# A token shift between two transformer blocks: from on-chip transfers to products with a shifted diagonal

## The chip, the cores and the metric

The program runs on one core of one Trainium2 chip. The metric is the device time of one execution in microseconds (us), as the median of several runs.

The engines, as the profile names them: PE (TensorE) multiplies matrices, PEld is its load of the stationary operand; DVE (VectorE) and ACT (ScalarE) compute element by element; POOL (GpSimd) does so too; SP (SyncE) only issues transfers. Each engine executes its own queue in order. SBUF is the on-chip memory of 128 partitions, PSUM the accumulators that PE writes.

## The reference, cut to what matters

Two blocks run one after the other on 256 tokens of width 1024. The second block has two layers; each begins with a mixer of four branches over one input projection, `x @ w_in`, and ends with a feed-forward (in layer 1 a mixture of eight experts). The second branch is recurrent, and it begins with a shift by one token: every token's 1024 projected columns are mixed with those of the token before it.

```python
def mixer_block(x, w_in, ...):
    p_swa, p_rwkv, p_fox, p_dsa, p_gate = split_cols(x @ w_in, IN_GROUPS)
    o_swa = swa_branch(*split_cols(p_swa, SWA_SPLITS), sinks)
    o_rwkv = rwkv7_branch(p_rwkv, mu, w0, w_up, ...)
    ...

def rwkv7_branch(p, mu, w0, w_up, a0, a_up, g_up, ...):
    p_prev = jnp.pad(p[:, :-1], ((0, 0), (1, 0), (0, 0)))
    p = p + mu * (p_prev - p)
    r, k, v, w_lo, a_lo, g_lo = split_cols(p, RWKV_SPLITS)
    ...
```

## The kernel before, in words

Activations lie token-major in two blocks of 128 tokens, t = 0 and 1, a token to a partition. A product (`gemm_tok`, L289) streams its weight from DRAM in pieces of at most 2048 columns. `wload` (L217) takes a piece into a buffer of the ring `raw` (three buffers, issued on SP, L222), and splits it in two parts: ACT casts the high part `whi` (L230), DVE subtracts it from the piece for the remainder `wlo` (L233). Each has a ring of four buffers. PE then makes three products per 128 rows of the weight: high by high (L323), remainder by the input's high part (L324), high by the input's low part (L325). So PE waits for ACT and DVE, these wait for the loads, and a new load waits for the remainder made from the buffer it will overwrite.

The mixer (`block2_mixer`, L1475) first projects the recurrent branch's 1024 columns, `p_rwkv`; `proj` evacuates them from the accumulators, block 0 by DVE (L1495), block 1 by ACT (L1493). Next come the projection of `p_swa` (768 columns, two banks of 384), two gates of 1024 columns and the other projections. The branches themselves are generators: `later` (L526) queues one, and `step` (L530) runs a piece of it whenever the products have consumed some weight, so their instructions stand between the products on each engine. The order on an engine comes from the order in which the program is written and from priorities that the framework gives; it is fixed when the program is built.

The recurrent branch (`rwkv`, L1194) has two tiles `pv`, one per block, for the token before. A memset clears row 0 of the first (L1205); three transfers on ACT's queue then move `p_rwkv` down by one partition: rows 0 to 126 of block 0 (L1206), its last row into row 0 of block 1 (L1207), and rows 0 to 126 of block 1 (L1208). When they have landed, L1219 subtracts, L1220 multiplies by `mu`, L1221 adds: for columns 768 to 1023 (the low-rank parts) all on DVE, for columns 0 to 767 the subtraction on DVE and the rest on POOL. The low-rank parts go through two activations (L1223, L1224) and a tensor-scalar (L1225), are transposed on PE (L1067, into `loT`), and multiplied by the small weights `ups` (L1237 to L1239). Later steps are `kk` and `sq` on POOL (L1271, L1273), which share that queue with `dup` (L1079) of the `p_swa` branch.

`mi` (L143) gives one of four PSUM banks for all such small products. The identity matrix for the transposes, `identr`, is a constant of 128x128 (L95 to L99). For the mixture of experts `moe_loads` (L1673) loads the router's weight `rw` and the constants `tri` and `iota` into a pool of that stage; `iota` is compared with ranks in L1776.

Of the kernel before, what the change touches and what calls it, by code (L numbers as in the profile page):

```python
# [26 lines left out]
def host_constants():  # L27
    c = {}
    c["ident"] = np.eye(P)
# [40 lines left out]
# small vectors of a layer of the second block, laid side by side  # L70
# [4 lines left out]
def layout(inputs):  # L75
    """The arrays of the launch: the inputs, and some of them once more laid out for fewer transfers."""
# [8 lines left out]
class Net:  # L85
    def __init__(self, ctx, tc, a, out, dump=None):
# [8 lines left out]
        self.identr = self.cp.tile([P, P], F32R, name="identr")  # L95
        self.ident = self.identr.bitcast(F32)
        t = self.sp.tile([P, 512], F32, name="c_ident", tag="xt", bufs=3)[:, :P]
        self.nc.gpsimd.dma_start(t, a["consts"][:, COFF["ident"][0]:sum(COFF["ident"])])
        self.nc.vector.tensor_copy(self.identr, t)  # L99
# [12 lines left out]
    def in_turn(self, dst, src):  # L112
        """A load behind the ones of the weights that came before it."""
        self.tc.keep_in_program_order(self.nc.sync.dma_start(dst, src))
# [31 lines left out]
    @staticmethod  # L146
    def staged(items):
        """items: lists of as many emitters; stage s of an item comes along with stage 0 of the s-th next. A generator."""
        n = len(items[0])
        for i in range(len(items) + n - 1):  # L150
            for s in range(n):
                if 0 <= i - s < len(items):
                    items[i - s][s]()
            yield

    def pipeline(self, items):
        for _ in self.staged(items):
            pass

    def rsqrt(self, v, n):  # L160
        """1/sqrt(v) for a [P, n] tile of float32."""
# [14 lines left out]
    def rsqrt1(self, v):  # L176
        """1/sqrt(v) for a tile [P, 3] of v, v / 4, v / 16: steps w' = (w w v / s - 3) w, with s the square of w's own
        factor, -2 for each; the last takes the factor -8 out."""
# [22 lines left out]
    def ring(self, tag, shape, dt):  # L201
        """A tile of the ring of that tag; more_rings, of (pool, slots by tag), add to it."""
# [9 lines left out]
    def prefetch(self, w, c0, cw, n=1):  # L212
        """Loads and splits the first n pieces of the weight of the next product ahead of their turn."""
# [3 lines left out]
    def wload(self, src, n, cw, f0):  # L217
        """Loads a piece of a weight, n columns from f0 on of its rows of cw laid end to end, and splits it in two
        float32r parts; a list of (row, first column, end, hi, lo) with hi(column, width), lo(column, width)."""
# [21 lines left out]
    def plan(w, c0, cw):  # L241
        """w: list of [P, nk, N] views; pieces of at most 2048 columns: whole rows, or any part of rows that lie end to end."""
# [16 lines left out]
    def pieces(self, w, c0, cw, pre=None):  # L259
        """Yields the parts of the pieces; pre() is traced after the first, and the vector engine's part  # L260
        of the second queues behind it."""
# [27 lines left out]
    def gemm_tok(self, lhs, w, c0, cw, toks, evac, tail=1, head=1, pre=None, nxt=None):  # L289
        """Token-major product: out[t] [128, cw] = sum_k lhs(k, t)^T w[k]; evac(t, column, width, psum).  # L290
        Through the first head and last tail pieces of the weight the first block of tokens goes ahead; pre(t) comes
        before the first use of block t; nxt: weight, column and width of the next product, to be loaded ahead."""
# [7 lines left out]
        for i, parts in enumerate(self.pieces(w, c0, cw, pre is not None and (lambda: pre(toks[0])))):  # L300
            # the last piece for the blocks behind the first one
# [32 lines left out]
    def gemm_feat(self, rhs, w, c0, cw, evac, pre=None):  # L334
        """Feature-major product: out[j] [128, 512 tokens] for each 128 columns of w; evac(j, psum). With pre the
        first two pieces go by halves of the tokens, and pre(half) comes before the first use of a half."""
# [35 lines left out]
    def turn4(self, z, K, k0):  # L372
        """Transposes of z [P, K*128] by feature = K*p + k, for four k's at most from k0 on."""
# [5 lines left out]
    def to_feat(self, z, K, hi, lo, affine=None, turned=None):  # L379
        """z [P, K*128] token-major -> hi/lo [P, K, 128] with feature = K*p + k.  # L380
        affine(k) -> (scale, shift) per-feature columns; shift may be None."""
# [20 lines left out]
    def rms_sum(self, ss, src, h, junk):  # L402
        """ss[:, h] <- sum of the squares of half h of src."""
# [10 lines left out]
    def rms_z(self, src, out):  # L414
        """out <- src [P, D] / its root mean square."""
# [6 lines left out]
    def close_rms(self, hs, gate, z):  # L422
        """evacuation of a residual product: hs[t] += gate(t) * product, then z(t) <- hs[t] / its root mean square."""
# [12 lines left out]
    def ln_var(self, st):  # L436
        """mean, and variance and eps in the form of rsqrt1, of the statistics st of the two halves."""
# [28 lines left out]
    def busy(self, n):  # L466
        """n products that nothing needs, which keep the tensor engine's clock up while loads are waited for."""
# [4 lines left out]
    def ada_lambda(self):  # L472
        nc, a = self.nc, self.a
        # lambda of the differential attention on all partitions
# [15 lines left out]
    def ada(self, l, s, norm=None):  # L490
        """mods[l, s] [P, 8, 2] <- segment s of the modulation of layer l, feature-major, for c and c_ctx;
        with norm: (1 + it) times that gain. A generator, one piece of the weight per step."""
# [37 lines left out]
    def step(self, n=1):  # L530
        """Runs n steps (may be a fraction, which adds up) of the work that was put off."""
# [12 lines left out]
    def gate_rows(self, l, s, c, out):  # L544
        """out [P, D] <- mods[l, s] of condition c on all partitions, by way of DRAM."""
# [1442 lines left out]
```

## Time and profile before

| | us |
|---|---|
| median of 3 runs | 2547.35 |
| lowest, highest run | 2543.98, 2552.41 |
| span of the profiled execution | 2546.3 |
| PE busy | 2356.2 (93%) |
| DVE busy | 1497.3 (59%) |
| ACT busy | 1065.1 (42%) |
| POOL busy | 298.6 (12%) |
| mean granted clock of PE | 0.953 of 2.4 GHz |

The span reaches from the first to the last instruction of one profiled execution; its own time as a run is not given apart from it, and the span lies within the range of the three runs. Busy shares are averages over stages with different limits; which wait ends last is read from the chain and the timelines. In a timeline row stand the start, the duration, the engine, the line, the operation, what it writes and reads, how many such rows were merged, and in brackets the idle time before it and what ended that.

### The profile page before, as it was taken

To read this page: it belongs to the slowest core of one execution; us is meant where nothing else is said; L and a number is where in the kernel's file an instruction comes from. 1 tells how busy PE (TensorE), PEld (TensorE's weight loads), DVE (VectorE), ACT (ScalarE), POOL (GpSimd) and SP (SyncE) were. 2 spreads that over 40 slices of the span, in tenths; PEclk is the share of its full clock that TensorE was granted. 3 is DMA by queue.
4 is the path that set the end of the run, shared out by engine and by line. 5 is a ranking of instruction groups with operands and counts; after the bars stand their busy time and mean duration, and the time that the engine had idled before them with its cause. 6 is when DMAs were issued, how large, how long until landed. Compare 5 with 4: busy or idle time off the path is not lost.

```text
span 2546.3 us, 33113 instructions
## 1 busy us (share of the span) xinstructions
PE 2356.2 (93%) x13136; PEld 1900.2 (75%) x13138; DVE 1497.3 (59%) x2473; ACT 1065.1 (42%) x1684; POOL 298.6 (12%) x242
## 2 busy tenths in 40 slices
PE   8899999999998999975999989974999979999996
PEld 4567877777776878854787768864787768889885
DVE  4247732322366565455566765464566778898887
ACT  3137432222235544432354344422344437666773
POOL 1100000000002000012101210022100322122222
PEclk8899999999999999997999999986999989999998
DMA  8581344544331065523244445622334438888994
GB/s 285 149 198 60 99 146 136 174 149 141 116 111 59 26 235 165 203 98 114 93 133 156 156 160 164 208 97 86 114 108 155 157 114 321 298 320 289 333 336 161
DMA packets 122067, 421.47 MB, mean 166 GB/s; under 512 B 11060, under 2 KB 16180, under 8 KB 100912
## 3 DMA queue, kind: packets, MB, share of 16 engines
q1 hardware_dynamic: 114128, 401.32, 45.8%
q0 software_dynamic: 4816, 15.27, 2.3%
q10 hardware_dynamic: 2960, 2.68, 0.3%
q8 instruction: 105, 1.72, 0.3%
q14 instruction: 58, 0.48, 0.1%
HBM read 416.08 MB, written 1.07 MB: 164 GB/s over the span
## 4 chain that ended last, share of the span: by engine, by line
PE 79%; DVE 9%; DMA 4%; issue 3%; POOL 2%; ACT 1%; ACTq 1%; SPq 0%; POOLq 0%; DVEq 0%
PE acc L323 17%; PE acc L324 17%; PE acc L325 17%; PE acc L356 3%; PE acc L357 3%; PE acc L358 3%; DMA pv<-p_rwkv 3%; DVE wlo L233 2%; PE mi L1029 2%; PE mi L517 2%; PE mi L506 2%; PE mi L1336 1%; PE mi L376 1%; PE mi L1784 1%; PE mi L985 1%
## 5 line engine op out<-in xcount | busy, mean ns | idle before, releaser
L233 DVE TENSOR_TENSOR wlo<-raw,whi 128x1024 fp32r<-128x1024 f32 (+2 forms) x648 | 802.1, 1262 | 495.9 <-ACT whi L230 493.5
L230 ACT CAST whi<-raw 128x1024 fp32r<-128x1024 f32 (+2 forms) x692 | 672.8, 1010 | 792.5 <-PE acc L325 574.5
L324 PE MATMUL acc<-wlo,xh 128*128 128x512 f32 (+3 forms) x1184 | 463.5, 392 | 81.4 <-DVE wlo L233 81.3
L323 PE MATMUL acc<-whi,xh 128*128 128x512 f32 (+3 forms) x1184 | 466.9, 399 | 28.0 <-ACT whi L230 22.3
L325 PE MATMUL acc<-whi,xl 128*128 128x512 f32 (+3 forms) x1184 | 460.1, 389 | 1.0 <-DVE xl L370 1.0
L324 PEld LDWEIGHTS acc<-wlo,xh 128*128 128x128 f32 x1184 | 230.4, 195 | 127.9 <-DVE wlo L233 91.9
L323 PEld LDWEIGHTS acc<-whi,xh 128*128 128x128 f32 x1184 | 230.5, 195 | 78.0 <-ACT whi L230 23.9
L325 PEld LDWEIGHTS acc<-whi,xl 128*128 128x128 f32 x1184 | 229.8, 194 | 39.5 <-issue 2.4
L324 PE MATMUL acc<-wlo,hh 128*128 128x512 f32 x528 | 208.9, 396 | 0.0
L323 PE MATMUL acc<-whi,hh 128*128 128x512 f32 x528 | 208.9, 396 | 0.0
L325 PE MATMUL acc<-whi,hl 128*128 128x512 f32 x528 | 208.3, 395 | 0.3 <-DVE hl L370 0.3
L323 PE MATMUL acc<-whi,gh 128*128 128x384 f32 (+3 forms) x512 | 172.8, 337 | 2.0 <-DVE yl L1848 2.0
L325 PE MATMUL acc<-whi,gl 128*128 128x384 f32 (+3 forms) x512 | 170.3, 333 | 0.0
L324 PE MATMUL acc<-wlo,gh 128*128 128x384 f32 (+3 forms) x512 | 170.0, 332 | 0.0
L233 POOL TENSOR_TENSOR wlo<-raw,whi 128x1024 fp32r<-128x1024 f32 x44 | 108.7, 2470 | 344.7 <-ACT whi L230 344.7
L356 PE MATMUL acc<-xh,whi 128*128 128x512 f32 (+1 forms) x384 | 148.0, 387 | 0.0
L357 PE MATMUL acc<-xl,whi 128*128 128x512 f32 (+1 forms) x384 | 147.2, 384 | 0.0
L358 PE MATMUL acc<-xh,wlo 128*128 128x512 f32 (+1 forms) x384 | 147.0, 384 | 0.0
L323 PEld LDWEIGHTS acc<-whi,hh 128*128 128x128 f32 x528 | 100.0, 189 | 26.5 <-issue 4.2
L325 PEld LDWEIGHTS acc<-whi,hl 128*128 128x128 f32 x528 | 100.1, 190 | 22.7 <-DVE hl L370 0.7
L324 PEld LDWEIGHTS acc<-wlo,hh 128*128 128x128 f32 x528 | 99.9, 189 | 21.6
L323 PEld LDWEIGHTS acc<-whi,gh 128*128 128x128 f32 x512 | 97.0, 189 | 11.4 <-DVE yl L1848 2.5
(574 smaller groups left out, 3225.9 us busy)
## 6 DMA issues: line engine op xcount, KB each, us to landing
raw<-in_exp_w_dram SPq DMA_DIRECT2D x120, 1024.0 KB, 5.8
raw<-in_ada_w_dram SPq DMA_DIRECT2D x48, 1024.0 KB, 5.2
raw<-in_w_in_dram SPq DMA_DIRECT2D x40, 1024.0 KB, 4.9
raw<-in_ffn_w_in_dram SPq DMA_DIRECT2D x32, 1024.0 KB, 5.2
raw<-in_ffn_w_dram SPq DMA_DIRECT2D x27, 1024.0 KB, 4.9
raw<-in_ffn_w_out_dram SPq DMA_DIRECT2D x19, 1024.0 KB, 5.0
raw<-in_exp_w_dram SPq DMA_DIRECT2D x24, 512.0 KB, 4.8
raw<-in_even_w_in_dram SPq DMA_DIRECT2D x10, 1024.0 KB, 5.4
```

What stands on the lines that cost most here:

```text
L230: nc.scalar.copy(hi, s)
L233: e.tensor_tensor(out=lo, in0=s, in1=hi.bitcast(F32), op=OP.subtract)
L323: nc.tensor.matmul(o, xh, hi(c, m), start=k == 0, stop=False)
L324: nc.tensor.matmul(o, xh, lo(c, m), start=False, stop=False)
L325: nc.tensor.matmul(o, xl, hi(c, m), start=False, stop=k == K - 1 and c + m == b + bw)
L356: nc.tensor.matmul(o, wh, xh[:, n0:n1], start=k == 0, stop=False)
L357: nc.tensor.matmul(o, wh, xl[:, n0:n1], start=False, stop=False)
L358: nc.tensor.matmul(o, wl, xh[:, n0:n1], start=False, stop=k == K - 1)
L376: self.nc.tensor.transpose(pt[:, j * P:(j + 1) * P], z[:, k0 + j::K], self.ident)
L506: nc.tensor.matmul(ps[32 * j:32 * j + 32, :], self.ct[:, 4 * g + j, :], v[:, j, :], start=g == 0, stop=g == 1, tile_position=(0, 32 * j))
L517: nc.tensor.matmul(pf[rw, 2 * k:2 * k + 2], mod[:, k::KD], self.sel2, start=True, stop=True, tile_position=(0, 64 * h))
L1029: nc.tensor.matmul(po[:, (h - c0) * 64:(h - c0) * 64 + 64], aT[:, j * P:(j + 1) * P], v(h, jj), start=jj == 0, stop=jj == nkb - 1)
```

## The change

The constant `ident` becomes `diag`, 128x264, with ones on a diagonal that starts at column 8. Three windows of it are used: from column 8 on the identity as before; from column 7 on a diagonal shifted by one (`shift[0]`); from column 135 on a matrix with a single one (`shift[1]`), which takes the last row of block 0 to the first row of block 1. The memset and the three transfers are gone. A new inner function `shifted` multiplies parts of `p_rwkv` by these windows in float32 into a bank of `mi`, and the subtraction reads that bank: 1 bank for columns 768 to 1023 of both blocks, 3 banks for the rest. The windows and the subtractions of columns 0 to 767 are cut to what fits a bank, so there are nine products and six subtractions per layer. All subtractions of a group of columns come ahead of its multiplications.

Two small edits go with it: the router's weight is loaded into a buffer of the ring `xt`, and `iota` is kept in bfloat16, loaded by way of the same ring and cast. (The diff also drops comments, so that lines of the changed kernel have other numbers; these are left out here.)

```diff
-    c["ident"] = np.eye(P)
+    c["diag"] = np.eye(P, P + 136, 8)
...
-        self.identr = self.cp.tile([P, P], F32R, name="identr")
+        diag = self.cp.tile([P, P + 136], F32R, name="diag")
+        t = self.sp.tile([P, 512], F32, name="c_diag", tag="xt", bufs=3)[:, :P + 136]
+        self.nc.gpsimd.dma_start(t, a["consts"][:, COFF["diag"][0]:sum(COFF["diag"])])
+        self.nc.vector.tensor_copy(diag, t)
+        self.identr = diag[:, 8:8 + P]
         self.ident = self.identr.bitcast(F32)
-        t = self.sp.tile([P, 512], F32, name="c_ident", tag="xt", bufs=3)[:, :P]
-        self.nc.gpsimd.dma_start(t, a["consts"][:, COFF["ident"][0]:sum(COFF["ident"])])
-        self.nc.vector.tensor_copy(self.identr, t)
+        self.shift = [diag[:, i:i + P].bitcast(F32) for i in (7, 7 + P)]
...
         pvs = [big("pv") for _ in range(2)]
-        nc.vector.memset(pvs[0][0:1, :], 0.0)
-        nc.scalar.dma_start(pvs[0][1:P, :], pr[0:P - 1, 0, :])
-        nc.scalar.dma_start(pvs[1][0:1, :], pr[P - 1:P, 0, :])
-        nc.scalar.dma_start(pvs[1][1:P, :], pr[0:P - 1, 1, :])
+        def shifted(*cols):
+            ps, o, out = self.mi(), 0, []
+            for t, c0, c1 in cols:
+                d = ps[:, o:o + c1 - c0]
+                nc.tensor.matmul(d, self.shift[0], pr[:, t, c0:c1], start=True, stop=t == 0)
+                if t:
+                    nc.tensor.matmul(d, self.shift[1], pr[:, 0, c0:c1], start=False, stop=True)
+                out.append((t, slice(c0, c1), d))
+                o += c1 - c0
+            return out
...
-        for c, eng in ((slice(768, 1024), nc.vector), (slice(0, 768), nc.gpsimd)):
+        for banks, eng in (([((0, 768, 1024), (1, 768, 1024))], nc.vector),
+                           ([((0, 0, 512),), ((1, 0, 512),), ((0, 512, 768), (1, 512, 768))], nc.gpsimd)):
+            for t, c, prev in [x for cols in banks for x in shifted(*cols)]:
+                nc.vector.tensor_tensor(out=pvs[t][:, c], in0=prev, in1=pr[:, t, c], op=OP.subtract)
+            c = slice(768, 1024) if eng is nc.vector else slice(0, 768)
             for t in (0, 1):
                 pv, p = pvs[t][:, c], pr[:, t, c]
-                nc.vector.tensor_tensor(out=pv, in0=pv, in1=p, op=OP.subtract)
                 eng.tensor_tensor(out=pv, in0=pv, in1=mu[:, c], op=OP.mult)
                 eng.tensor_tensor(out=p, in0=p, in1=pv, op=OP.add)
...
-        rw = pool.tile([P, KD, E], F32, name="rw")
+        rw = self.sp.tile([P, 512], F32, name="rw", tag="xt", bufs=3)[:, :KD * E].rearrange("p (k e) -> p k e", k=KD)
...
-        tri, iota = (self.const(n, pool) for n in ("tri", "iota"))
+        tri, iota = self.const("tri", pool), self.maskb("iota", pool)
```

How the change moves instructions is seen at three places; both layers read alike. On DVE, behind the evacuation of `p_rwkv`, the order before is the following (L1219 to L1221 are the shift's arithmetic, L233 the weight remainders, L1225 and L1073 the low-rank parts on their way to `loT`).

```order
L1495 COPY p_rwkv<-acc 128x512 x2
L1219 TENSOR_TENSOR pv<-pv,p_rwkv 128x256
L1219 TENSOR_TENSOR pv<-pv,p_rwkv 128x768
L1220 TENSOR_TENSOR pv<-pv,mu_8396 128x256
L1221 TENSOR_TENSOR p_rwkv<-p_rwkv,pv 128x256
L233 TENSOR_TENSOR wlo<-raw,whi 128x768 x2
L1219 TENSOR_TENSOR pv<-pv,p_rwkv 128x256
L1219 TENSOR_TENSOR pv<-pv,p_rwkv 128x768
L1220 TENSOR_TENSOR pv<-pv,mu_8396 128x256
L233 TENSOR_TENSOR wlo<-raw,whi 128x768
```

In the changed kernel the same place on DVE reads so (L236 is the remainder's new number, L1230, L1234 and L1235 are the shift's arithmetic, L1239 and L1076 the low-rank parts).

```order
L1509 COPY p_rwkv<-acc 128x512 x2
L236 TENSOR_TENSOR wlo<-raw,whi 128x768 x4
L1230 TENSOR_TENSOR pv<-mi,p_rwkv 128x256 x2
L1234 TENSOR_TENSOR pv<-pv,mu_8396 128x256 x2
L1235 TENSOR_TENSOR p_rwkv<-p_rwkv,pv 128x256 x2
L1230 TENSOR_TENSOR pv<-mi,p_rwkv 128x512
L1239 TENSOR_SCALAR p_rwkv<-p_rwkv 128x2x128
L1230 TENSOR_TENSOR pv<-mi,p_rwkv 128x512
L1230 TENSOR_TENSOR pv<-mi,p_rwkv 128x256 x2
L1076 COPY loT<-mi 128x2x128
L236 TENSOR_TENSOR wlo<-raw,whi 128x768 x2
```

Four of the six remainders that stood between and behind the first subtractions now stand ahead of all of them, and two behind the copy of `loT`.

On PE nothing of the shift stood in the queue before: behind the 24th product of `p_swa` (128x384) came four products with the high part and then one with a remainder.

```order
L323 MATMUL acc<-whi,xh 128x384 x4
L324 MATMUL acc<-wlo,xh 128x384
L325 MATMUL acc<-whi,xl 128x384
L323 MATMUL acc<-whi,xh 128x384
L324 MATMUL acc<-wlo,xh 128x384
```

Now the nine products of the shift stand there in two groups, three behind the 24th product of `p_swa` and six behind the 36th; this is the second group with the rows about it (L326 to L328 are the weight products).

```order
L328 MATMUL acc<-whi,xl 128x384
L1214 MATMUL mi<-p_rwkv,diag 128x512 x2
L1216 MATMUL mi<-p_rwkv,diag 128x512
L1214 MATMUL mi<-p_rwkv,diag 128x256 x2
L1216 MATMUL mi<-p_rwkv,diag 128x256
L326 MATMUL acc<-whi,xh 128x384
```

Twelve weight products follow it, then the four transposes for `loT`, twelve more, and the low-rank products; before, the transposes came in pairs after 28 and 35 products behind the 24th, and the low-rank products after 41.

On POOL the branch's operations stood so before (layer 0; L1079 copies a part of `p_swa`).

```order
L1220 TENSOR_TENSOR pv<-pv,mu_8396 128x768
L1221 TENSOR_TENSOR p_rwkv<-p_rwkv,pv 128x768
L1079 COPY dup<-p_swa 128x2x64
L1271 TENSOR_TENSOR kk<-p_rwkv,vec_6724 128x512
L1079 COPY dup<-p_swa 128x2x64
L1273 TENSOR_TENSOR sq<-kk 128x512
```

In the changed kernel, in layer 1, they read as follows (L1234 and L1235 are the shift's arithmetic, L1285 and L1287 `kk` and `sq`, L1082 the copies).

```order
L1690 DMA rw<-in_router_w_dram 128x64
L128 DMA c_iota<-in_consts_dram 128x128
L1234 TENSOR_TENSOR pv<-pv,mu_12943 128x768 x2
L1235 TENSOR_TENSOR p_rwkv<-p_rwkv,pv 128x768 x2
L1285 TENSOR_TENSOR kk<-p_rwkv,vec_12717 128x512
L1082 COPY dup<-p_swa 128x2x64
L1287 TENSOR_TENSOR sq<-kk 128x512
```

The two multiplications and two additions now stand together, `kk` stands ahead of the first copy, and in layer 1 two loads that were issued at the mixer's end stand ahead of them all.

## Rows read from the trace of the kernel before

**Rows 1.** The page: span, and the chain that ended last by engine and by line.
```profile
span 2546.3 us, 33113 instructions
...
PE 79%; DVE 9%; DMA 4%; issue 3%; POOL 2%; ACT 1%; ACTq 1%; SPq 0%; POOLq 0%; DVEq 0%
PE acc L323 17%; PE acc L324 17%; PE acc L325 17%; PE acc L356 3%; PE acc L357 3%; PE acc L358 3%; DMA pv<-p_rwkv 3%; DVE wlo L233 2%; PE mi L1029 2%; PE mi L517 2%; PE mi L506 2%; PE mi L1336 1%; PE mi L376 1%; PE mi L1784 1%; PE mi L985 1%
```
**Rows 2.** The chain in order of time: start, duration (us), what.
```profile
1136.66 37.07 DMA pv<-p_rwkv
...
1717.22 37.53 DMA pv<-p_rwkv
```
**Rows 3.** The tile pv: idle time of the waiting engine (us, times) until.
```profile
  DMA pv<-p_rwkv: 80.6, 4
```
**Rows 4.** Timeline of DVE, layer 0.
```profile
1150.06 1.29 DVE L1219 TENSOR_TENSOR pv<-pv,p_rwkv 128x256 f32<-128x256 f32 x2 [23.76 <-DMA pv<-p_rwkv]
...
1153.55 3.42 DVE L233 TENSOR_TENSOR wlo<-raw,whi 128x768 fp32r<-128x768 f32 x2
1173.76 1.29 DVE L1219 TENSOR_TENSOR pv<-pv,p_rwkv 128x256 f32<-128x256 f32 x2 [16.79 <-DMA pv<-p_rwkv]
```
**Rows 5.** Timeline of PE, layer 0: first and last of 24 products, and later.
```profile
1128.11 0.34 PE L323 MATMUL acc<-whi,xh 128*128 128x384 f32 x1
...
1132.09 0.34 PE L325 MATMUL acc<-whi,xl 128*128 128x384 f32 x1
...
1156.15 0.69 PE L324 MATMUL acc<-wlo,xh 128*128 128x384 f32 x1 [16.24 <-DVE wlo L233]
...
1184.60 0.48 PE L1237 MATMUL mi<-ups,loT 64*128 64x256 f32 x1
...
1186.84 0.53 PE L325 MATMUL acc<-whi,xl 128*128 128x384 f32 x1
```
**Rows 6.** Timeline of PE, layer 1: the same two ends of the run.
```profile
1713.64 0.34 PE L325 MATMUL acc<-whi,xl 128*128 128x384 f32 x1
...
1769.06 0.53 PE L325 MATMUL acc<-whi,xl 128*128 128x384 f32 x1
```
**Rows 7.** A 10 us stretch: busy time (instructions) by engine, clock, DMA share, GB/s.
```profile
1140.00:1150.00 10.00, 0.00 (x0) 0.00 (x0) 0.00 (x0) 0.41 (x1) 0.00 (x0) 0.50 0.06 26
```
**Rows 8.** Timeline of PE: nearest rows for the products and the transposes.
```profile
174.00 3.27 PE L676 MATMUL mi<-kT,qT 64*128 64x512 f32 x8
...
179.97 1.13 PE L676 MATMUL mi<-kT,qT 64*128 64x512 f32 x4
...
1106.12 1.14 PE L376 MATMUL mi<-identr,xstate 128*128 128x128 f32 x8 [1.24 <-DVE xstate L412]
...
1188.47 1.13 PE L1252 MATMUL mi<-lw,c_up_incl 128*128 128x256 f32 x4
1189.43 0.95 PE L1256 MATMUL mi<-c_up_incl,lw 128*128 128x2 f32 x8
```
**Rows 9.** Timeline of DVE: a tensor-tensor that reads PSUM.
```profile
1186.60 0.69 DVE L1240 TENSOR_TENSOR lw<-mi,vec 128x512 f32<-128x512 f32 x1 [2.78 <-PE mi L1238]
```
**Rows 10.** Timelines of POOL and DVE side by side, layer 0.
```profile
1175.13 1.92 POOL L1220 TENSOR_TENSOR pv<-pv,mu 128x768 f32<-128x768 f32 x1 [19.85 <-DVE pv L1219]
1177.13 2.41 POOL L1221 TENSOR_TENSOR p_rwkv<-p_rwkv,pv 128x768 f32<-128x768 f32 x1
...
1175.31 2.56 DVE L233 TENSOR_TENSOR wlo<-raw,whi 128x768 fp32r<-128x768 f32 x1
```
**Rows 11.** Timelines of DVE and PE, layer 1, in the product that follows.
```profile
1779.65 0.69 DVE L1275 TENSOR_REDUCE kks<-sq 128x8 f32<-128x512 f32 x1 [2.43 <-POOL sq L1273]
...
1784.22 0.51 PE L324 MATMUL acc<-wlo,xh 128*128 128x512 f32 x1 [1.62 <-DVE wlo L233]
```
**Rows 12.** Issues of loads (KB each, us to landing), and instructions of L1776 (ns).
```profile
raw<-in_w_in_dram SPq DMA_DIRECT2D x4, 768.0 KB, 4.4
...
L1776 DVE TENSOR_SCALAR G<-c_iota,rk x16: 266/277/1830, 2073.8 to 2287.6; 128x128 fp32r<-128x128 f32 x16
```

## The prediction, made before the changed kernel ran

> **What bounds the kernel now.** The page comes first: the chain that ended last is PE for 79%, so what PE computes and what it waits for set the time, and among the chain's lines stands one that is no computation, the transfer pv<-p_rwkv with 3% [rows 1]. Followed in order of time, the chain goes through that transfer twice, 37.07 us from 1136.66 and 37.53 us from 1717.22 [rows 2]: once per layer of the second block. The view of the tile pv says who stood still: DVE sat idle 80.6 us in 4 waits until those transfers had landed [rows 3]. DVE's own timeline shows why that matters. From 1126.3 on it has nothing, for 23.76 us, until the first shifted block is there; does its few operations and two weight remainders (wlo, L233); and waits 16.79 us more for the second block [rows 4]. The remainders were not late themselves: they queue behind L1219.
>
> PE needs them. In layer 0 its 24th product of the p_swa projection starts at 1132.09; the product at 1156.15 has waited 16.24 us for wlo, and there is a second such wait after DVE's second one. At 1186.84 PE has done 41 more products of this projection, four transposes of p_rwkv and the low-rank products L1237 to L1239, and goes on without a pause [rows 5]. In layer 1 the same run reaches from 1713.64 to 1769.06 [rows 6]. The stretches show the price twice over: from 1140 to 1150 PE is busy for 0.00 us, DMA moves 26 GB/s, and the granted clock is 0.50, the lower of its two levels, 1.2 GHz, so the products that follow the idle time take longer too [rows 7].
>
> **What goes.** The memset and three transfers per layer go. With them goes DVE's wait, the ACT queue's time for issuing them, and PE's wait behind both. How long PE would need for the same work without a wait gives the gain:
>
> - p_swa products: 24 of them start 3.98 us apart, first to last [rows 5], so 0.173 us each; the one at the stretch's start and the 41 after it are 42 x 0.173 = 7.3 us.
> - Four transposes at 1.14 / 8 = 0.14 us [rows 8]: 0.6 us.
> - L1237 to L1239, 1184.60 to 1186.84 [rows 5]: 2.2 us. The ups they read are loaded by POOL as before.
>
> **What is added.** Per layer PE gets nine products with the shifted diagonal, in float32: six of 256 columns, three of 512. The first kind is in the trace: two products of 128x256 in float32 (L1252) take from 1188.47 to 1189.43 [rows 8], 0.48 us each, so 2.9 us. The second isn't there with 128 rows. Nearest is L676, 64 rows by 512 columns, two products side by side: 1.13 us a pair in one place, and 3.27 us for two pairs, 1.63 each, in another [rows 8]. So a product costs between 0.57 (half a pair) and 1.63 us; I take 2 x 0.48 = 0.96, twice the columns of the nearest row, hence 2.9 us, with bounds 1.7 and 4.9. Together 5.8 us of PE per layer, all on the path, since PE is what bounds the new stretch.
>
> The Trainium skill (FP8 and Floating Point Precision, TensorE Precision Notes) says that true FP32 takes 4 passes through the array. An estimate from that page, four times 512 columns at 2.4 GHz, is 0.85 us, and 0.43 for 256, or 5.1 us per layer in place of 5.8. The L1252 row is above it, 0.48 against 0.43, so the row is used.
>
> DVE's six subtractions per layer now read PSUM, which in this trace costs a 512-column tensor-tensor 0.69 us (L1240) [rows 9]; before they were four instructions of the same columns. Their sum is under 4 us in a stretch where DVE waits anyway, so nothing. The order puts four remainders ahead of the first subtraction: those PE needs next are made before DVE waits for a product. DVE then waits for PE at four places, with two remainders behind the last (the loT copy); PE needs these only 24 products later, about 4 us. The products need no data that is late: both blocks of p_rwkv are evacuated before PE reaches them. PSUM: all four mi buffers are taken by the nine products, each freed by a DVE subtraction; the transposes behind them come 12 products, 2.1 us, later.
>
> New stretch, layer 0: 7.3 + 0.6 + 2.2 + 5.8 = 15.9 us, in place of 1186.84 - 1132.09 = 54.75: 38.9 less. Layer 1: 55.42 - 15.9 = 39.5 less. I give back 0.5 us per layer for hand-overs between engines: 77.4 us. The granted clock goes with it: with PE no longer idle it need not leave its upper level here.
>
> The rest of the change. The longer constant (264 columns, not 128) is one load and one cast at the program's start. The router's weights and iota move ahead in POOL's queue of layer 1, ahead of POOL's four operations of the shift; two issues while POOL has nothing else. In bfloat16 iota is read by 16 instructions of 266 to 277 ns [rows 12]; half or double of that is 4 us at most on an engine that is not the bound there. All these: 0, with ±2 us in the range.
>
> **Sum.** The profiled execution spans 2546.3 us [rows 1]; less 77.4 is 2468.9. The span is 1.05 us below the median of the runs, 2547.35, so about **2470 us**.
>
> **Rivals.**
>
> *DVE keeps part of it.* POOL now does its four 128x768 operations back to back, 1.9 to 2.4 us each, about 8 us. Next to POOL a remainder took 2.56 us, ending 0.8 us after POOL's multiplication did [rows 10]. If the two remainders behind the loT copy wait all of this out and PE has no work in hand, up to 7.6 us per layer come back: 2485 us. Against it: PE has 24 products and L1237 to L1239 in hand, some 6 us. The Trainium skill (SBUF — State Buffer, Who interferes with whom) has it that a DVE instruction with two SBUF inputs and a GpSimd instruction that reads SBUF lock each other out for a whole instruction. By that rule the 2.56 us is POOL's rest plus the remainder itself, as the rows show, and this rival's place is exactly there.
>
> *More goes than I count.* At 1784.22 PE waited 1.62 us for a remainder, whose engine had stood 2.43 us for POOL's sq [rows 11]. POOL's order now has kk ahead of the first dup, which waits for the projection's end; sq is then ready earlier. Up to 2.4 us per layer, 5 us in all: 2465 us.
>
> *The weights become the wait.* Loads of 768 KB land 4.4 us after issue [rows 12], and a ring of three buffers is refilled only as remainders are made. If each of the next product's four pieces came one landing late, 4 x 4.4 x 2 = 35 us would return: 2505 us. Against it: 26 GB/s in the stall leaves the DMA engines nearly empty, and no row above shows PE or DVE waiting for a weight's load.
>
> *Slower: the products cost more than the transfers.* Eighteen products stand in PE's queue, and everything behind them waits. From 77.4 + 11.6 = 89 us in all, 4.9 us each, the gain is gone; at 6 us each the kernel takes 2566 us. No float32 row of up to 512 columns comes near: 1.63 us is the worst.
>
> *Nothing happens.* If the remainders stayed behind the subtractions and these behind something as late, the time would stay at 2547. The new order speaks against it.
>
> **How the numbers follow.** Forecast 0.67; DVE keeps part 0.14; more goes 0.13; weights 0.03; nothing 0.015; slower 0.015. A change of 0.3%, 7.6 us, is about what a measurement of this kernel can tell from none. The first four are all faster by more than that: 0.97; same 0.015; slower 0.015. The range starts from 2470. Down: 2.4 us for 512-column products at their lower bound, 5 for the second rival, 5 for the spread of the runs and the small edits: 2458. Up: 15 for the first rival, 4 for the products at their upper bound (3 x 0.67 us x 2): 2488. Outside are the weights and the last two rivals.
>
> **What would show it.** No pv<-p_rwkv transfer in the chain; PE's stretches behind the 24th p_swa product about 16 us long up to the end of L1239's counterpart; the nine products at 0.48 and about 0.96 us; granted clock at 1.00 throughout; DVE's longest wait there a few us, for PE. The forecast is wrong if PE again stands for wlo for over 5 us per layer, or if a new wait for a raw load or for mi stands in these stretches.

## The result, and the profile after

| | before | changed |
|---|---|---|
| median of the runs, us | 2545.66 (4 runs) | 2467.68 (4 runs) |
| span of the profiled execution, us | 2546.3 | 2464.3 |
| PE busy, us (share) | 2356.2 (93%) | 2353.4 (95%) |
| mean granted clock | 0.953 | 0.969 |

The ratio is 0.9695, with a 95% interval from 0.9678 to 0.9711: 78.0 us less. The forecast was 2470 us, within 2458 to 2488. A fourth run of the hybrid, in the table of experiments, took 3042 us at a granted clock of 0.695 and is left out there.

The page of the changed kernel, chain by engine and by line (to be laid beside [rows 1]):

```profile
span 2464.3 us, 33187 instructions
...
PE 84%; DVE 9%; issue 2%; ACT 2%; POOL 1%; DMA 1%; SPq 0%; ACTq 0%; POOLq 0%; DVEq 0%
PE acc L326 18%; PE acc L327 18%; PE acc L328 18%; PE acc L359 4%; PE acc L360 3%; PE acc L361 3%; DVE wlo L236 3%; PE mi L1032 2%; PE mi L520 2%; PE mi L509 2%; PE mi L1350 2%; PE mi L379 1%; PE mi L1798 1%; PE mi L988 1%; PE mi L1016 1%
```

The transfer is out of the chain, and PE's share rose from 79 to 84%. In the view of the tile pv, which engine sat idle until what ended it (us, times), DVE's idle time for the shift went from 80.6 us in 4 waits [rows 3] to:

```profile
  PE mi L1216: 2.8, 4
```

PE's timeline of layer 0 answers to [rows 5]: 24 products of p_swa, the shift's products (L1214, L1216), the transposes, the low-rank products, and the product that follows them.

```profile
1120.00 0.34 PE L326 MATMUL acc<-whi,xh 128*128 128x384 f32 x1
...
1124.07 0.34 PE L328 MATMUL acc<-whi,xl 128*128 128x384 f32 x1
1124.24 1.03 PE L1214 MATMUL mi<-p_rwkv,diag 128*128 128x256 f32 x4
1125.10 0.60 PE L1216 MATMUL mi<-p_rwkv,diag 128*128 128x256 f32 x2
...
1127.65 1.88 PE L1214 MATMUL mi<-p_rwkv,diag 128*128 128x512 f32 x4
1129.37 1.02 PE L1216 MATMUL mi<-p_rwkv,diag 128*128 128x512 f32 x2
1130.23 1.03 PE L1214 MATMUL mi<-p_rwkv,diag 128*128 128x256 f32 x4
...
1133.64 0.60 PE L1070 MATMUL mi<-diag,p_rwkv 128*128 128x128 f32 x4
...
1136.29 0.48 PE L1251 MATMUL mi<-ups,loT 64*128 64x256 f32 x1
...
1138.53 0.53 PE L326 MATMUL acc<-whi,xh 128*128 128x384 f32 x1
```

No row has a wait. The stretches (us; length; busy us of PE, PEld, DVE, ACT, POOL with instructions; granted clock, DMA share, GB/s) are alike in both layers:

```profile
1124.07:1138.53 14.46, 14.46 (x73) 11.42 (x72) 10.68 (x16) 3.86 (x7) 6.30 (x4) 1.00 0.38 139
1671.66:1686.12 14.46, 14.46 (x72) 11.41 (x72) 10.70 (x16) 3.87 (x7) 6.30 (x4) 1.00 0.38 140
```

PE is busy throughout, at 2.4 GHz. Before, the same ends were 54.75 and 55.42 us apart [rows 5, 6], and in layer 0 PE was busy for 15.46 us of it at a mean granted clock of 0.63:

```profile
1132.09:1186.84 54.75, 15.46 (x59) 12.44 (x59) 16.41 (x17) 5.57 (x9) 8.10 (x4) 0.63 0.20 69
```

Now 36 products of p_swa stand between the ends, before 41. To compare equal work, one follows both kernels to the first remainder product of the next projection (before 1194.72 and 1776.94; here the changed kernel's):

```profile
1147.57 0.39 PE L327 MATMUL acc<-wlo,xh 128*128 128x512 f32 x1
...
1695.21 0.40 PE L327 MATMUL acc<-wlo,xh 128*128 128x512 f32 x1
```

From the 24th product on that is 62.63 and 63.30 us before, 23.50 and 23.55 now: 39.1 and 39.8 us, **78.9 in both layers**. The two executions also differ by 8.0 us ahead of the first of these stretches (1132.09 against 1124.07), where nothing of the shift stands. About 7 us of it are weight products of 512 columns in the first 850 us, which start 0.2279 us apart in the mean and before 0.2312; of the change only the wider constant stands ahead of them, and the experiments come back to it. Other differences go both ways, so a single execution is no measure of a few us.

### The profile page after: what moved, and what is told of

Its sections match the earlier page's. It is cut to its first block, busy times and chain, and to the rows that moved or that the text cites. A ratio compares the mean times of both kernels' runs of the same rounds, so it can differ in the third digit from the quotient of the medians.

```text
span 2464.3 us, 33187 instructions
## 1 busy us (share of the span) xinstructions
PE 2353.4 (95%) x13174; PEld 1903.9 (77%) x13174; DVE 1493.5 (61%) x2476; ACT 1064.8 (43%) x1684; POOL 299.0 (12%) x242
## 4 chain that ended last, share of the span: by engine, by line
PE 84%; DVE 9%; issue 2%; ACT 2%; POOL 1%; DMA 1%; SPq 0%; ACTq 0%; POOLq 0%; DVEq 0%
PE acc L326 18%; PE acc L327 18%; PE acc L328 18%; PE acc L359 4%; PE acc L360 3%; PE acc L361 3%; DVE wlo L236 3%; PE mi L1032 2%; PE mi L520 2%; PE mi L509 2%; PE mi L1350 2%; PE mi L379 1%; PE mi L1798 1%; PE mi L988 1%; PE mi L1016 1%
## 5 line engine op out<-in xcount | busy, mean ns | idle before, releaser
L236 DVE TENSOR_TENSOR wlo<-raw,whi 128x1024 fp32r<-128x1024 f32 (+2 forms) x648 | 802.1, 1263 | 507.4 <-ACT whi L233 505.0
L233 ACT CAST whi<-raw 128x1024 fp32r<-128x1024 f32 (+2 forms) x692 | 673.0, 1010 | 741.5 <-PE acc L328 541.8
L326 PE MATMUL acc<-whi,xh 128*128 128x512 f32 (+3 forms) x1184 | 466.0, 397 | 18.6 <-ACT whi L233 12.4
L328 PE MATMUL acc<-whi,xl 128*128 128x512 f32 (+3 forms) x1184 | 458.6, 388 | 3.4 <-DVE xl L373 3.4
L326 PEld LDWEIGHTS acc<-whi,xh 128*128 128x128 f32 x1184 | 227.9, 193 | 68.2 <-ACT whi L233 13.4
L328 PEld LDWEIGHTS acc<-whi,xl 128*128 128x128 f32 x1184 | 227.7, 192 | 43.3 <-DVE xl L373 5.3
L326 PE MATMUL acc<-whi,hh 128*128 128x512 f32 x528 | 209.2, 396 | 0.0
L328 PE MATMUL acc<-whi,hl 128*128 128x512 f32 x528 | 208.4, 395 | 0.3 <-DVE hl L373 0.3
L326 PE MATMUL acc<-whi,gh 128*128 128x384 f32 (+3 forms) x512 | 172.8, 338 | 1.8 <-DVE yl L1862 1.8
L328 PE MATMUL acc<-whi,gl 128*128 128x384 f32 (+3 forms) x512 | 170.4, 333 | 0.0
L236 POOL TENSOR_TENSOR wlo<-raw,whi 128x1024 fp32r<-128x1024 f32 x44 | 108.6, 2467 | 343.9 <-ACT whi L233 343.9
L326 PEld LDWEIGHTS acc<-whi,hh 128*128 128x128 f32 x528 | 100.2, 190 | 26.4 <-issue 4.2
L328 PEld LDWEIGHTS acc<-whi,hl 128*128 128x128 f32 x528 | 100.2, 190 | 22.5 <-DVE hl L373 0.7
L326 PEld LDWEIGHTS acc<-whi,gh 128*128 128x128 f32 x512 | 97.2, 190 | 11.2 <-DVE yl L1862 2.3
```

The lines of the kernel that those rows point to most:

```text
L233: nc.scalar.copy(hi, s)
L236: e.tensor_tensor(out=lo, in0=s, in1=hi.bitcast(F32), op=OP.subtract)
L326: nc.tensor.matmul(o, xh, hi(c, m), start=k == 0, stop=False)
L328: nc.tensor.matmul(o, xl, hi(c, m), start=False, stop=k == K - 1 and c + m == b + bw)
```

## The experiments

Times are medians, ratios go to the kernel before in the same series of runs. The transfers, where a kernel has them, are as before unless the diff says otherwise.

| run | median, us | ratio, 95% interval |
|---|---|---|
| small edits alone | 2553.1 | 1.0027 (1.0016 to 1.0038) |
| layer 0 only | 2508.2 | 0.9849 (0.9831 to 0.9866) |
| split transfer | 2476.7 | 0.9715 (0.9689 to 0.9742) |
| DVE free | 2548.9 | 1.0015 (1.0000 to 1.0030) |
| products doubled | 2477.5 | 0.9735 (0.9719 to 0.9750) |
| hybrid (three runs) | 2467.2 | 0.9710 (0.9690 to 0.9730) |
| hybrid, late | 2468.7 | 0.9705 (0.9689 to 0.9721) |
| late only | 2463.4 | 0.9678 (0.9661 to 0.9696) |
| router's edits only | 2545.0 | 1.0006 (0.9995 to 1.0017) |
| identity at column 0 | 2552.4 | 1.0028 (1.0016 to 1.0040) |
| **constant of 256 columns** | **2457.7** | **0.9655 (0.9642 to 0.9668)** |
| constant of 256, late | 2458.4 | 0.9661 (0.9648 to 0.9675) |

**Is the gain the wait, layer by layer?** In `e2_layer0_only` the function has both ways in:

```diff
+        if L == 1:
+            nc.vector.memset(pvs[0][0:1, :], 0.0)
+            nc.scalar.dma_start(pvs[0][1:P, :], pr[0:P - 1, 0, :])
...
```

> Products in layer 0, transfers in layer 1. My theory (each layer's wait is paid for by itself): half of the 78 us comes back, 2467.7 + 39 = 2507 us, within 5 us, and layer 1's stretch is 55 us long again while layer 0's stays at 14.5 us. Rival (one layer's wait was partly hidden, or what layer 0 gains is given back before layer 1): over 2515 or under 2499 us.

It took 2508.2 us, 1 us from the theory. Its two stretches:

```profile
1125.09:1139.55 14.46, 14.46 (x72) 11.41 (x72) 10.70 (x16) 3.87 (x7) 6.31 (x4) 1.00 0.37 137
1670.89:1726.02 55.13, 16.98 (x59) 13.86 (x59) 16.41 (x17) 5.57 (x9) 8.08 (x4) 0.60 0.20 73
```

Each layer pays for itself.

**Is it late data, or DVE's order?** `e4_dve_free` takes the shift's arithmetic off DVE in the kernel before:

```diff
-                nc.vector.tensor_tensor(out=pv, in0=pv, in1=p, op=OP.subtract)
-                eng.tensor_tensor(out=pv, in0=pv, in1=mu[:, c], op=OP.mult)
+                nc.gpsimd.tensor_tensor(out=pv, in0=pv, in1=p, op=OP.subtract)
+                nc.gpsimd.tensor_tensor(out=pv, in0=pv, in1=mu[:, c], op=OP.mult)
...
```

> The kernel before, its transfers untouched, with all twelve operations of the shift and the scaling behind the tanh on POOL instead of half of them on DVE, so that no weight remainder queues behind a subtraction that waits for a transfer. Theory (the data is late for PE too: its transposes of p_rwkv stand in its queue behind 21 more products): PE waits at the transposes instead of at wlo, 2530 to 2555 us. Rival (what costs is DVE's order alone): 2500 us or less.

2548.9 us: no gain. PE no longer stands for wlo; it stands in one piece at the transposes (layer 0):

```profile
1176.29 0.48 PE L1067 MATMUL mi<-identr,p_rwkv 128*128 128x128 f32 x1 [38.43 <-ACT p_rwkv L1223]
```

So the queue behind L1219, which the prediction put first, was only where the lateness showed. With it gone the next waiter on the same transfer takes its place.

**What made the transfer slow?** `e3_split_transfer` changes the two large transfers alone:

```diff
-        nc.scalar.dma_start(pvs[0][1:P, :], pr[0:P - 1, 0, :])
+        nc.scalar.dma_start(pvs[0][1:113, :], pr[0:112, 0, :])
+        nc.scalar.dma_start(pvs[0][113:P, :], pr[112:P - 1, 0, :])
...
```

> The kernel before, with each transfer of 127 partitions made as two, of 112 and of 15 partitions. Theory (the wait is the 20 us that half a MB takes at some 26 GB/s, because a transfer of 127 partitions runs on a single DMA engine): 112 and 15 partitions spread over more engines, a block lands in some 3 to 6 us, about the time of a 768 KB weight load (4.4 us), and the time falls to 2465 to 2490 us without any product. Rival (a transfer from SBUF to SBUF is slow on any number of engines, or the place of the subtractions in DVE's queue is what costs): 2520 us or more.

2476.7 us: 69 of the 78 us come back without a product. The view of the transfers gives each kind of piece its size and its median time from issue to landing (first two lines). In the view of the tile pv, DVE waits for them 14.0 us in 2 waits, against 80.6 in 4 [rows 3], and all pieces together land so:

```profile
pv<-p_rwkv ACTq DMA_DIRECT2D x4, 448.0 KB, 5.2
pv<-p_rwkv ACTq DMA_DIRECT2D x4, 60.0 KB, 4.4
...
  DMA pv<-p_rwkv: 14.0, 2
...
DMA to landing us min/median/max: 1.9/5.0/9.0
```

At 26 GB/s [rows 7] the 448 KB of 112 partitions alone would take 17.6 us; they landed after 5.2. So the rate hung on the partition count, and not on the way from SBUF to SBUF: the 127 partitions moved at 26 GB/s with 0.06 of the DMA engines' time busy, about one engine in 16. The 37.07 us of [rows 2] are more than one such transfer, for the first block landed only at 1150.06 [rows 4] and the second, issued at 1136.66, came behind it. Other cuts than 112 and 15 were not tried. The Trainium skill (DMA: Bandwidth & Descriptors, Why a DMA increments its semaphore by 16 and not by 1) says that the number of DMA engines of a transfer is the largest up to 16 that divides the size of its slowest dimension: one for 127 partitions, 16 for 112, 15 for 15. The split run agrees: its pieces land 1.9 to 9.0 us after their issue. The 9 us to the changed kernel are not clear of noise, as the two intervals overlap. In the profile, which is of the slowest of the four runs (2485.8 us), what is left against the products stands on PE. A remainder comes late, because it stands on DVE behind the shift's arithmetic, and that has waited 9.25 us for the first block; here DVE's order does matter:

```profile
1140.69 0.69 PE L324 MATMUL acc<-wlo,xh 128*128 128x384 f32 x1 [6.77 <-DVE wlo L233]
```

**What do the products cost?** `e5_products_doubled`:

```diff
-        self.shift = [diag[:, i:i + P].bitcast(F32) for i in (7, 7 + P)]
+        self.shift = [diag[:, i:i + P].bitcast(F32) for i in (7, 7 + P, 8 + P)]
...
-                nc.tensor.matmul(d, self.shift[0], pr[:, t, c0:c1], start=True, stop=t == 0)
+                nc.tensor.matmul(d, self.shift[0], pr[:, t, c0:c1], start=True, stop=False)
+                nc.tensor.matmul(d, self.shift[2], pr[:, t, c0:c1], start=False, stop=t == 0)
...
```

> The changed kernel with each of its nine products per layer followed by one of the same shape with a block of zeros, which adds nothing to the sum. From the trace of the changed kernel the nine take 4.8 us (three of 512 columns from 1127.65 to 1130.23, three of 256 from 1130.23 to 1131.33, three more of 256). If PE bounds the stretch: 2 x 4.8 = 9.6 us more, 2477 us, and stretches of 19.3 us in place of 14.5. If other engines' work covers products (the hybrid, with six of nine products gone, gained nothing): the doubled ones would be covered in part too, under 2472 us.

2477.5 us, 9.8 more. The stretches grew by 5.17 us:

```profile
1130.05:1149.67 19.62, 19.62 (x90) 14.82 (x90) 10.83 (x16) 3.86 (x7) 6.30 (x4) 1.00 0.28 103
1677.76:1697.40 19.64, 19.64 (x91) 14.84 (x90) 10.83 (x16) 3.87 (x7) 6.30 (x4) 1.00 0.28 101
```

That is three products of 0.86 and six of 0.43, 5.16 us; the 4.8 of the expectation had the last product of each group too short, as the rows of one group end where the next instruction starts. Added products are paid for in full.

**Are products that are taken away paid back?** `e6_hybrid` keeps three of the nine:

```diff
+        nc.sync.dma_start(pvs[0][1:113, 0:768], pr[0:112, 0, 0:768])
+        nc.sync.dma_start(pvs[0][113:P, 0:768], pr[112:P - 1, 0, 0:768])
...
-                           ([((0, 0, 512),), ((1, 0, 512),), ((0, 512, 768), (1, 512, 768))], nc.gpsimd)):
+                           ((), nc.gpsimd)):
...
+                if not banks:
+                    nc.gpsimd.tensor_tensor(out=pv, in0=pv, in1=p, op=OP.subtract)
```

> The changed kernel, with products for the 256 low-rank columns alone; the other 768 come by transfers of 112, 15 and 1 partitions in SP's queue, and POOL subtracts. If the path of the new kernel is PE's work in the stretch, six of the nine products go: 2 x (2.58 + 1.1) = 7.4 us less, 2460 us. Rival (the transfers delay the weight loads behind them in SP's queue, or POOL's six operations of some 2 us make kk and sq late): 2468 us or more.

2467.2 us: nothing gained, though in these stretches no wait of PE for a load shows. The six products that went are 3.9 us per layer. The stretches hold the same 36 products of p_swa as in the changed kernel and take 14.40 and 20.75 us (columns as above):

```profile
1122.36:1136.76 14.40, 12.53 (x61) 10.60 (x60) 11.31 (x13) 3.86 (x7) 10.31 (x5) 0.88 0.48 159
1668.10:1688.85 20.75, 13.32 (x61) 11.10 (x60) 14.66 (x13) 3.75 (x7) 12.00 (x7) 0.75 0.42 149
```

PE waits at the transposes, 0.78 and 1.09 us in layer 0 and 7.27 in layer 1, and behind the wait the granted clock falls to 1.2 GHz for a while: products of 384 columns then start 0.32 us apart. In layer 0 the two together eat what the six products gave; in layer 1 of this execution they cost 6 us more. The low-rank chain on DVE stretched, in layer 1 most, beside POOL's operations (DVE, then POOL):

```profile
1674.12 3.31 DVE L1242 TENSOR_TENSOR pv<-pv,mu 128x256 f32<-128x256 f32 x2
1677.35 3.42 DVE L1243 TENSOR_TENSOR p_rwkv<-p_rwkv,pv 128x256 f32<-128x256 f32 x2
...
1672.68 2.53 POOL L1241 TENSOR_TENSOR pv<-pv,p_rwkv 128x768 f32<-128x768 f32 x1
1675.29 1.86 POOL L1242 TENSOR_TENSOR pv<-pv,mu 128x768 f32<-128x768 f32 x1
1677.23 1.86 POOL L1243 TENSOR_TENSOR p_rwkv<-p_rwkv,pv 128x768 f32<-128x768 f32 x1
```

In the changed kernel the same DVE operations take 0.42 us each, and POOL starts only after them. So the six products there hold POOL back and give PE work while that chain runs; this is read from the traces, and no run holds POOL back without the products. `e7_hybrid_late` moves the transposes one step later, and `e10_late_only` does the same to the changed kernel:

```diff
+        yield
         loT = two("loT")
```

> The hybrid (products for the low-rank columns alone, the rest by split transfers in SP's queue, POOL subtracts) with the transposes of p_rwkv one step later: 36 p_swa products ahead of them, not 24. In the hybrid PE waited 0.78 and 1.09 us at the transposes for ACT's tanh and DVE's scaling behind it. If that wait is all that ate the hybrid's 7.4 us: 2460 to 2464 us. If the low-rank chain only ends later for what follows (lw, the decays), 2467 us or more.

> Control: the changed kernel with the transposes of p_rwkv one step later and nothing else. In it PE does not wait at the transposes, so 2467.7 us within 3.

The late hybrid took 2468.7 us. PE still waits 2.89 and 1.09 us at the transposes of layer 0, and the same DVE operations take 1.4 to 2.1 us (one addition 0.41). The control gave 2463.4 us, below the 2467.7 within 3 that was expected; its interval overlaps that of the changed kernel, so this is not told from no change.

**The small edits.** `e1_small_edits` is the changed kernel with the memset, the three transfers and the subtraction of before put back:

```diff
+        nc.vector.memset(pvs[0][0:1, :], 0.0)
+        nc.scalar.dma_start(pvs[0][1:P, :], pr[0:P - 1, 0, :])
...
-            for t, c, prev in [x for cols in banks for x in shifted(*cols)]:
-                nc.vector.tensor_tensor(out=pvs[t][:, c], in0=prev, in1=pr[:, t, c], op=OP.subtract)
...
+                nc.vector.tensor_tensor(out=pv, in0=pv, in1=p, op=OP.subtract)
```

> The change without its core: the wider constant, the router's weights in the xt ring and iota in bfloat16 stay, but the shift is made by the memset and the three transfers as before. My theory (the gain is the two waits for the transfers): the time of before, 2545.7 us, within 4 us. Rival (the small edits, which also move POOL's issues and the loads of the last stage, carry part of the 78 us): 2535 us or less.

2553.1 us: they cost 7 us (by the interval 4 to 10), which neither theory had. Two runs look for the part. `e8_router_only` is the kernel before with the edits of `rw` and `iota` as in the diff further up; `e9_identity_at_0` changes the run of the small edits:

```diff
-    c["diag"] = np.eye(P, P + 136, 8)
+    c["diag"] = np.eye(P, P + 136)
...
-        self.identr = diag[:, 8:8 + P]
+        self.identr = diag[:, :P]
```

> The kernel before with the edits of the router's weights (xt ring) and of iota (bfloat16) alone; constant and transfers as before. The small edits together cost 7 us. If these two carry it: 2550 to 2555 us. If it is the wider constant that holds the identity (the clock fell earlier beside the products with foxc and the identity in both layers, and layer 0 comes ahead of the router's loads): 2546 us within 2.

> As the run of the small edits (2553 us, transfers as before), but the identity stands in columns 0 to 127 of the wide constant, not 8 to 135. If the place of the identity in its tile is what the small edits' 7 us hang on: 2546 us within 2. If it is the width of the constant or merely where the instructions come to lie in time: 2550 us or more.

2545.0 and 2552.4 us: not the router's edits, and not the identity's place in its tile. So the width of the constant, 264 columns, is left. And the profiles have a mark of it: in the changed kernel 24 products of p_swa start 4.07 us apart, first to last (above), before 3.98 [rows 5], and all kernels with the 264 columns are on the one side, all without on the other. `e11_constant_256` packs the same windows into 256 columns; every engine's order is the same as in the changed kernel:

```diff
-    c["diag"] = np.eye(P, P + 136, 8)
+    c["diag"] = np.eye(P, 2 * P, 1)
...
-        self.identr = diag[:, 8:8 + P]
+        self.identr = diag[:, 1:1 + P]
...
-        self.shift = [diag[:, i:i + P].bitcast(F32) for i in (7, 7 + P)]
+        self.shift = [diag[:, i:i + P].bitcast(F32) for i in (0, P)]
```

> The changed kernel with a constant of 256 columns, not 264 (the identity from column 1, the two shift matrices from 0 and 128); every engine's order is the same. In all kernels with 264 columns products of 384 columns start 0.1765 us apart, in all without it 0.1735, and those of 354 columns 0.165 against 0.162. Theory (8 columns of 4 bytes put every later tile of SBUF 32 bytes further, and PE reads such tiles a little slower; the 7 us of the small edits hang on that): the pitch goes back to 0.1735, and the time to 2460 us, within 3. Rival (the pitch and the 7 us come from the constant being there at all, or from instructions' places in time): 2465 us or more, pitch 0.1765.

**2457.7 us**, 10 us less than the changed kernel, with intervals that do not meet: this version beats both. Its first and last of the 24 products are 3.99 us apart:

```profile
1125.74 0.33 PE L326 MATMUL acc<-whi,xh 128*128 128x384 f32 x1
...
1129.73 0.34 PE L328 MATMUL acc<-whi,xl 128*128 128x384 f32 x1
```

The mark is not the cost, though. Products of 512 columns moved both ways: in the first 850 us they start 0.2279 us apart in the mean with the small edits alone and 0.2312 before, from there to 2000 us 0.2317 and 0.2295. Summed over neighbouring weight products that run at the upper clock in both traces, the small edits alone lose 0.7 us by it in the whole kernel.

The cost hangs on the clock. Where the third branch's products with `foxc` (4 rows) and with its keys (64 rows) run, 30 us from their start, PE is busy all the time in every kernel, but at another granted clock: layer 0 and 1 of the small edits alone, then of the constant of 256 columns.

```profile
1331.00:1361.00 30.00, 30.00 (x112) 20.57 (x112) 14.72 (x27) 11.01 (x27) 0.87 (x2) 0.72 0.55 193
1917.50:1947.50 30.00, 30.00 (x112) 20.69 (x112) 14.74 (x27) 11.02 (x27) 0.92 (x2) 0.72 0.53 193
```

```profile
1286.90:1316.90 30.00, 30.00 (x136) 21.82 (x136) 16.53 (x30) 12.84 (x29) 0.86 (x2) 0.89 0.53 193
1825.80:1855.80 30.00, 30.00 (x136) 21.96 (x136) 16.49 (x30) 12.86 (x29) 0.91 (x2) 0.89 0.54 193
```

In equal time 112 instructions of PE come through in the first, 136 in the second. The kernel before has 0.89 in both layers, as the constant of 256 has; the changed kernel 0.77 and 0.89. With 0.72 the clock falls to 1.2 GHz twice in the stretch, with 0.89 once, and the products with `foxc`, first to last, take 20 us and not 16. Of the 10.2 us by which the span of the small edits alone exceeds that of the kernel before, 8.0 lie in these two places. This is not a strict mark of the constant: layer 1 of the split transfer, which has the constant of before, shows 20 us and 0.72 too.

The granted clock of all runs, not of the profiled ones alone, says the same. Its mean was 0.950 with the small edits alone (0.948 to 0.952 in ten runs) and 0.954 before (0.951 to 0.956 in 19); 0.9675 in the changed kernel (0.966 to 0.969) and 0.971 with 256 columns (0.969 to 0.973). Time multiplied by the granted clock, averaged over the runs, is 2426 us against 2427, and 2388 against 2387. So the cost of the eight columns is time at the lower clock; why the clock falls more with them no run shows. `e12_constant_256_late` adds the later transposes:

> The same with the transposes of p_rwkv one step later, which alone gave 2463.4 us, 4 us less than the changed kernel. If both gains are real and independent: 2456 us within 3. If the later transposes' 4 us were the place of a fall of the clock: as the run with 256 columns alone, within 2 us.

2458.4 us lies within both of its cases (2456 within 3, and 2457.7 within 2) and decides nothing between them. No gain by the later transposes can be told here.

## Why the prediction was right, step by step

- **What bounds the kernel.** Right. No pv<-p_rwkv in the chain, stretches at clock 1.00, DVE's idle time for the shift 2.8 us in 4 waits, no wait of PE for wlo, raw or mi in them. "The remainders were not late themselves: they queue behind L1219" is true of the rows, but less than the cause: with DVE free PE waited 38.43 us for the same data. Why the transfers took so long the prediction did not ask; it was their 127 partitions.
- **What goes and what is added.** 15.9 us were forecast for a stretch, 14.46 measured, with five p_swa products (0.9 us) fewer in it: 15.3 for equal work. The mis-sized term is the nine products, 5.8 us, measured 5.2: 0.43 and 0.86 us each in place of 0.48 and 0.96. The profile has four instructions for the pair of L1252 [rows 8]. The first, which comes after a short pause of PE, starts 0.32 us ahead of the second, and from there on they start 0.22 apart; those of the shift's products of 256 columns, without a pause, are 0.22 apart throughout. That is 1.2 us in both layers. The upper bound of 1.63 us came from a row at another clock: from 174.00 to 177.27 the mean granted clock was 0.60, while it was 1.00 for the row with 1.13 us. The prediction's estimate from the Trainium skill's four passes (FP8 and Floating Point Precision, TensorE Precision Notes) was 0.43 and 0.85 us; these rows agree with it.
- **The gain.** 77.4 us forecast (78.4 less 1.0 of hand-overs); 78.9 measured to the next projection's first remainder product. The 0.5 us per layer given back for hand-overs between engines was not needed.
- **Small edits: 0, with ±2 us.** This step failed. They cost 7 us, by the constant's eight columns beyond 256, and the cost is time at the lower clock (0.950 in the mean against 0.954). The text looked at the constant's load and cast at the program's start, and not at what else its size moves. `iota` in bfloat16 cost nothing: its 16 instructions took 265 to 278 ns, against 266 and 277 [rows 12].
- **DVE keeps part of it.** The place of this rival was right, but its price was not paid: the two remainders behind the loT copy took 4.76 us beside POOL, and PE, with work in hand, did not wait for them.

```profile
1134.40 4.76 DVE L236 TENSOR_TENSOR wlo<-raw,whi 128x768 fp32r<-128x768 f32 x2
```

  The hybrid shows the same mechanism where PE does wait. Of it the Trainium skill (SBUF — State Buffer, Who interferes with whom) says that DVE with two SBUF inputs and POOL reading SBUF lock each other out for whole instructions; 0.42 us that became 1.7 in the mean beside POOL's operations of 1.9 to 2.5 us agree with it.
- **More goes than I count.** This came too, in part. PE's 1.62 us [rows 11] are gone, and in the same layer DVE's wait for sq went from 2.43 to 0.93 us:

```profile
1696.46 0.69 DVE L1289 TENSOR_REDUCE kks<-sq 128x8 f32<-128x512 f32 x1 [0.93 <-POOL sq L1287]
```

  From the next projection's first remainder product to the first product with `foxc` the changed kernel takes 1.9 and 1.7 us less than the small edits alone.
- **The sum.** 2470 against 2467.7 us is closer than the reasoning was, and that is luck: more was gained than forecast, and the constant took it back. 78.9 and 3.6 us of gain, less 7.0 for the constant, are 75.5; the remaining 2.5 us are within what one fall of the clock, more or less, moves (in the changed kernel layer 1 has the later fall alone). Without the constant's eight columns the same change gave 88 us, and the forecast would have been 12 us off, with the time just below its range. (The upper end, 2470 with 15 and 4, is 2489 and not 2488; nothing hangs on it.)
- **The weights become the wait; slower; nothing happens.** None came. The product price from which the change would have lost was 4.9 us, measured at most 0.86.

## What to carry to other kernels

A block of 128 partitions shifted by one is a transfer of 127; look at its rate before blaming its kind. Cutting 127 partitions into 112 and 15 gave 69 of 78 us without a product, and only then did the place of the waiting instruction in its engine's queue show as a wait of its own. What a product costs on the path can't be read as what its removal gives. Added ones were paid in full. Taking six away, with transfers and POOL's subtractions in their place, gave nothing: by the traces they had covered DVE's chain and held POOL back, and without them PE waited and its granted clock fell behind the wait. Price every edit beside the one in the title; here a constant that was eight columns wider than needed ate 10 us, and only a run with the side edits alone showed it. And when two kernels with the same order differ by a few us, compare the granted clock of all runs before looking for the cause in a single profile.

## What the runs showed of the hardware that was not expected

- A constant of 264 instead of 256 columns of 4 bytes, at the same order of instructions, changed how far apart products start, in all kernels that have it: those of 384 columns some 0.1765 us instead of 0.1735, those of 354 columns 0.165 instead of 0.162. Those of 512 columns came closer together in the first 850 us (0.2279 instead of 0.2312) and further apart from there to 2000 us (0.2317 instead of 0.2295). The eight columns move what lies behind them by 32 bytes in each partition; that this place is the cause was argued, not shown, and stays open.
- PE's clock fell to 1.2 GHz while PE was busy 30.00 of 30.00 us, after products with operands of 4 and 64 rows. One such fall more or less is worth about 4 us of this kernel. In six of the eight profiles with the constant of 264 columns there was one more, in one layer or both, and in one of the six without it. The 10 us of the constant are time at the lower clock (granted 0.9675 against 0.971 at nearly the same product of time and clock); why is open.
- A transfer of 508 KB between partitions of SBUF moved at 26 GB/s; cut into 112 and 15 partitions its pieces landed after 5.0 us in the median.
